# Chunk 5 of a squared-ReLU MLP as seven block products, with the splits of activations joined and two early weight loads

## The chip, the cores and the metric

The kernel runs on one core of one Trainium2 chip. The metric is the device time of one execution in microseconds (us), the median of several. The kernel before takes 505.07 us (three runs, 505.05 to 505.77). All times of single instructions come from one profiled execution of it, which took 505.25 us by itself; its span, from the first instruction to the last, is 503.5 us.

## The reference

One layer on 256 tokens of width 1024, all in float32: a conformer convolution and a sparse attention, mixed; a cross-attention on 256 memory tokens; an MLP with a squared ReLU; a final norm. Only the MLP is concerned here:

```
h  = h + CrossAttn(RMSNorm(h), RMSNorm(mem))
hf = RMSNorm(h) @ w_ff1            # 256 x 1024 times 1024 x 4096
h  = h + square(relu(hf)) @ w_ff2  # 256 x 4096 times 4096 x 1024
return RMSNorm(h)
```

## The kernel before

**Precision.** TensorE (PE) multiplies in fp32r, a rounded form of float32. Each operand is split into an upper part `hi` (a copy on ScalarE, ACT, that rounds) and the rest `lo` (a difference on VectorE, DVE). A product is three matmuls: hi by hi, hi by lo, lo by hi. So each weight of 1 MB (a chunk of 128 x 2048 numbers) costs DMA one load into a buffer `raw`, ACT two copies of 128x1024 and DVE two differences of 128x1024, ahead of the matmuls.

**Chunks.** The 4096 hidden columns are cut into 16 chunks of 256. For chunk c, `first(c, side)` makes its hidden values from the first weights `f1` of the chunk, one side (128 hidden columns) at a time: 24 matmuls into the PSUM bank `ps_f`. `activation` (a job in pieces, begun by `Hidden.after`) then applies Relu and Square and splits the result into `fs` (hi and lo). The second product, `half_of(c, half)`, multiplies it with the second weights `f2` of the chunk and adds into the banks `ps_p`, which hold sums over all chunks.

**Seven instead of eight.** The second product of a chunk is a 2 by 2 arrangement of blocks on each side of the product. Straightforwardly it takes eight block products of 512 columns, 24 matmuls. For the chunks in the table `SEVEN` it is done in the manner of Strassen and Winograd with seven, 21 matmuls. That needs sums of blocks of the weights (`sums`, made in `seven` by `outer` and `inner` on DVE and then split themselves) and differences of blocks of the activations (`fn`, in `activation`). The seven products take the weights in four pieces: `left` and `last` (parts of the weight itself), `outer` and `inner` (sums). Chunk 5 is not in the table before, so it takes eight, with two pieces 0 and 1 of the weight.

**The turn.** The loop over c up to 12 makes one turn out of `first(c + 2, 0)`, `half_of(c, 0)`, `first(c + 2, 1)`, `half_of(c, 1)`. Chunks 0 and 1 of `first` are made ahead of the loop.

**What sets the order.** All five instruction streams are written out by the program in the order of its calls; each engine does its own in that order and waits by semaphores. Weights come in the order `STREAM`: ..., f1 of chunks 0 and 1, f1 2, f2 0, f1 3, f2 1 and so on. Three buffers `raw` hold them; a load is issued on the queue of SyncE (SP) by `load()`, at the moment the last difference that reads an earlier one is written down (`high`, or the stage `inner` of `seven`). Its splits stand in `high_jobs` and `low_jobs`; `split_high` and `split_low` write out the next of each whenever `weights`, `split_ahead` or a tick between products asks. `HALVES` limits how many split halves may be there unused. A `Stage` has something to do `before` its copy (the sums); it is prepared when it stands second in line. The jobs of `activation` go on by one piece at each tick, each piece a few instructions up to its next `yield`.

**Memory and names.** `t8` and `w2` hand out work buffers from small rings; `cst` holds what stays. `raw51` to `raw53` are f1 of 0, 1 and 2, `raw54` is f2 of chunk 0; from there f1 and f2 alternate: `raw58` is f2 of chunk 2, `raw64` f2 of chunk 5, `raw70` f2 of chunk 8. In the kernel's listing, line 80 issues what DVE and PE do, 240 the copies of `seven`'s pieces, 263 the copies of other weights, 1166 the Relu straight from PSUM, 1170 and 1171 Relu and Square in place, 1190 the copy of the activations' upper parts, and 405 the copy of a bank whose sum is made in two banks (`merge`). Buffers such as `ki2`, `bias`, `score` and `zero_r` belong to earlier stages.

Of the kernel before, what the change touches and what calls it, by code (L numbers as in the profile page):

```python
# [16 lines left out]
P = 128  # L17
D = 1024
# [41 lines left out]
SEVEN = (2, 3, 4, 6, 7, 8, 9, 10, 11, 12)  # L60
JOINED = 13
BY_HALVES = tuple(("f1", i) for i in (4, 5, 6, 7))
# [52 lines left out]
def block_kernel(ctx, tc, x, xt, mem, memt, wst, wki, vecs, convw, gout, out):  # L115
# [23 lines left out]

    def bank(tag, bufs, name):  # L140
        return psum.tile([P, 512], F32, tag=tag, bufs=bufs, name=name)
# [19 lines left out]
    nload = [0]  # L161
    high_jobs, low_jobs = [], []

    def load(parts=1):
# [37 lines left out]
    class Stage:  # L202

        def __init__(self, key, high, before=None, slot=True):
            self.key, self.high, self.before, self.slot = key, high, before, slot
            if not slot:
                elsewhere.add(key)

        def prepare(self):
            if self.before:  # L210
                self.before()
                self.before = None

    def seven(key, c, raw):
# [15 lines left out]
        def stage(name, src_of, n, before=None):  # L230
            def high():
                src = src_of()
                if before:
# [16 lines left out]
            return Stage((*key, name), high, before, not before)  # L250

        return [stage("left", lambda: b[:, :, 0, :], 2), stage("last", lambda: flat[:, 3:4, :], 1),
                stage("outer", lambda: sums[0][:, 0:2, :], 2, outer), stage("inner", lambda: sums[0][:, 2:4, :], 2, inner)]

    def high(key, c, raw, ns, q, last):
# [184 lines left out]
    zero_r = cst.tile([P, 512], F32R, name="zero_r")  # L440
# [9 lines left out]
    ki2 = cst.tile([P, S], F32, name="ki2")  # L450
# [191 lines left out]
    bias = [cst.tile([P, P * (qb + 1)], F32, name=f"bias{qb}") for qb in range(2)]  # L642
# [22 lines left out]
    def index_scores():  # L665
# [4 lines left out]
        for qb in range(2):  # L670
            nk = P * (qb + 1)
            score = cst.tile([P, nk], F32, name=f"score{qb}")
# [490 lines left out]

    def activation(c, ct, ps, t, sh, sl):
        if ps.shape[1] == S:
            act(t[:, ct, :], ps, AF.Relu)  # L1166
        else:
            yield from merge(t[:, ct, :], ps)
            yield
            act(t[:, ct, :], t[:, ct, :], AF.Relu)  # L1170
        act(t[:, ct, :], t[:, ct, :], AF.Square)
        yield
        flat = t.rearrange("p k (r n) -> p (k r) n", r=2)
        if c not in SEVEN:
            cs = [(slice(2 * ct, 2 * ct + 2), flat[:, 2 * ct : 2 * ct + 2, :])]
        else:
            cs = [(slice(1, 3), flat[:, 2:4, :]) if ct else (slice(0, 1), flat[:, 0:1, :])]
        if ct and c < JOINED:
            n = w2(f"fn{c}", F32, (P, 4, P))
            if c in SEVEN:  # L1180
                dve.tensor_tensor(out=n[:, 0:2, :], in0=flat[:, 1:2, :].to_broadcast([P, 2, P]), in1=flat[:, 0:4:3, :],
                                  op=ALU.subtract)
                dve.tensor_tensor(out=n[:, 2, :], in0=flat[:, 0, :], in1=n[:, 1, :], op=ALU.subtract)
                dve.tensor_tensor(out=n[:, 3, :], in0=flat[:, 2, :], in1=n[:, 2, :], op=ALU.subtract)
                cs.append((slice(3, 7), n))
            else:
                dve.tensor_tensor(out=n[:, 0:2, :], in0=flat[:, 0:4:2, :], in1=flat[:, 1:4:2, :], op=ALU.subtract)
                cs.append((slice(4, 6), n[:, 0:2, :]))
        for js, src in cs:
            act(sh[:, js, :], src, AF.Copy)  # L1190
        yield
        for js, src in cs:
            dve.tensor_tensor(out=sl[:, js, :], in0=src, in1=sh[:, js, :].bitcast(F32), op=ALU.subtract)

    class Hidden:

        def __init__(self, c):
# [3 lines left out]
            self.t = w2(f"ft{c}", F32, (P, 2, S))  # L1201
# [7 lines left out]
        def row(self, k, rb):  # L1209
            return self.of(2 * k + rb)  # L1210
# [37 lines left out]
    TERMS = {"left": (("1", 0), ("2", 1)), "last": (("3", 6),), "outer": (("5", 4), ("7", 3)), "inner": (("6", 5), ("4", 2))}  # L1248
# [23 lines left out]
    def last_residual(rb, ps, lo, hi):  # L1272
        h = h_rm[:, lo // P : hi // P, rb, :]
        ps = by_tiles(ps)
        dve.scalar_tensor_tensor(out=h, in0=ps, scalar=r2[0][:, rb : rb + 1], in1=h, op0=ALU.mult, op1=ALU.add)

    def last_squares(rb, n, lo, hi):

        h = h_rm[:, lo // P : hi // P, rb, :]
# [163 lines left out]
```

## Time and profile before

| what | us |
|---|---|
| median of three runs | 505.07 |
| lowest and highest | 505.05, 505.77 |
| the profiled execution's own time | 505.25 |
| its span | 503.5 |

The profile's page gives for each engine the time it was busy (PE is TensorE's matmuls, PEld its weight loads, DVE VectorE, ACT ScalarE, POOL GpSimd), then the span in 40 slices, the DMA queues, and the chain of work that ended last. A row of a timeline reads: start, duration, engine, line, operation, output tile <- input tiles, partitions x elements and types, count; in brackets the engine's idle time just before it and what ended it. In it, rows with a count sum up neighbours of one form. A row of the chain of waits reads: start, duration, engine and what it did. Starts follow each other more closely than durations say, since instructions overlap by their beginnings and ends. A window row gives the busy time and the number of instructions for PE, PEld, DVE, ACT and POOL, then the granted clock of TensorE, the share of the DMA engines, and GB/s. The grouped rows give a group's count, its busy time with the mean in ns of one, and its idle time ahead. The lines are shown where the prediction uses them.

### The profile page before, as it was taken

To read this page: it belongs to the slowest core of one execution; us is meant where nothing else is said; L and a number is where in the kernel's file an instruction comes from. 1 tells how busy PE (TensorE), PEld (TensorE's weight loads), DVE (VectorE), ACT (ScalarE), POOL (GpSimd) and SP (SyncE) were. 2 spreads that over 40 slices of the span, in tenths; PEclk is the share of its full clock that TensorE was granted. 3 is DMA by queue.
4 is the path that set the end of the run, shared out by engine and by line. 5 is a ranking of instruction groups with operands and counts; after the bars stand their busy time and mean duration, and the time that the engine had idled before them with its cause. 6 is when DMAs were issued, how large, how long until landed. Compare 5 with 4: busy or idle time off the path is not lost.

```text
span 503.5 us, 8292 instructions
## 1 busy us (share of the span) xinstructions
PE 493.6 (98%) x3119; PEld 444.1 (88%) x3119; DVE 459.9 (91%) x858; ACT 349.1 (69%) x639; POOL 31.6 (6%) x49
## 2 busy tenths in 40 slices
PE   7999999999999999999999999999999999999995
PEld 5999998888888888888889999988989899988984
DVE  5999999999999799999988986888999899999994
ACT  7657777788656676668756667586777677777832
POOL 2002212221021100000000000000000000000000
PEclk9999999999999999999999999999999999999999
DMA  8949678899787744345645454368855645544602
GB/s 312 381 184 280 185 191 261 226 246 262 225 265 215 191 148 144 119 158 197 246 169 218 175 174 161 127 192 214 239 181 184 235 159 206 221 178 168 251 1 84
DMA packets 27225, 100.36 MB, mean 199 GB/s; under 512 B 10656, under 2 KB 11552, under 8 KB 17200
## 3 DMA queue, kind: packets, MB, share of 16 engines
q1 hardware_dynamic: 23120, 92.90, 53.4%
q0 software_dynamic: 3632, 6.59, 7.3%
q8 instruction: 24, 0.39, 0.3%
q10 hardware_dynamic: 432, 0.33, 0.2%
q14 instruction: 17, 0.14, 0.1%
HBM read 91.16 MB, written 1.05 MB: 183 GB/s over the span
## 4 chain that ended last, share of the span: by engine, by line
PE 62%; DVE 18%; ACT 7%; DMA 7%; issue 5%; POOLq 0%; POOL 0%; DVEq 0%; ACTq 0%
PE ps_conv L80 10%; DMA raw<-in_wst_dram 6%; PE ps_f L80 6%; DVE lo L80 5%; PE ps_ao L80 4%; PE ps_q L80 4%; PE ps_k L80 4%; PE ps_ga L80 4%; PE ps_gc L80 4%; PE ps_v L80 4%; PE ps_xo L80 3%; DVE sums L80 3%; PE ps_qi L80 2%; PE ps_xk L80 2%; PE ps_p L80 2%
## 5 line engine op out<-in xcount | busy, mean ns | idle before, releaser
L80 DVE TENSOR_TENSOR lo<-raw,hi 128x1024 fp32r<-128x1024 f32 x141 | 170.5, 1214 | 5.2 <-ACT hi L263 5.1
L263 ACT ACTIVATE hi<-raw 128x1024 fp32r<-128x1024 f32 x141 | 146.7, 1046 | 2.0 <-DMA raw<-in_wst_dram 2.0
L80 PE MATMUL ps_f<-ff_p,hi 128*128 128x256 f32 (+1 forms) x448 | 92.8, 299 | 0.6 <-ACT ft L1166 0.3
L80 DVE SCALAR_TENSOR_TENSOR acc<-u,cw,acc 128x234 f32<-128x234 f32 (+29 forms) x190 | 78.0, 461 | 0.3
L80 PEld LDWEIGHTS ps_f<-ff_p,hi 128*128 128x128 f32 x448 | 72.8, 191 | 5.8 <-ACT ft L1166 2.0
L80 PE MATMUL ps_f<-ff_p,lo 128*128 128x256 f32 x256 | 70.9, 282 | 0.0
L80 PEld LDWEIGHTS ps_f<-ff_p,lo 128*128 128x128 f32 x256 | 48.8, 191 | 0.6
L80 PE MATMUL ps_conv<-n_p,hi 128*128 128x256 f32 x224 | 41.0, 285 | 0.0
L80 PEld LDWEIGHTS ps_conv<-n_p,hi 128*128 128x128 f32 x224 | 34.9, 192 | 0.8 <-issue 0.7
L80 PE MATMUL ps_conv<-n_p,lo 128*128 128x256 f32 x112 | 31.7, 283 | 0.0
L588 POOL DMA_DIRECT2D acc<-products x25 | 21.6, 864 | 125.1 <-ACT products L587 50.1
L80 PE MATMUL ps_p<-hi,fs 128*128 128x512 f32 (+1 forms) x88 | 27.2, 372 | 0.0
L80 PE MATMUL ps_q<-n_p,hi 128*128 128x512 f32 x64 | 23.6, 406 | 0.0
L80 PE MATMUL ps_k<-n_p,hi 128*128 128x512 f32 x64 | 23.5, 407 | 0.0
L80 PE MATMUL ps_ao<-o_p,hi 128*128 128x512 f32 x64 | 22.6, 401 | 0.0
L80 PE MATMUL ps_co<-u_p,hi 128*128 128x512 f32 (+1 forms) x80 | 22.2, 351 | 0.0
L80 PE MATMUL ps_mix<-mix_p,hi 128*128 128x512 f32 (+1 forms) x80 | 22.2, 351 | 0.0
L80 PE MATMUL ps_ga<-n_p,hi 128*128 128x512 f32 x64 | 22.0, 396 | 0.0
L80 PE MATMUL ps_gc<-n_p,hi 128*128 128x512 f32 x64 | 22.0, 396 | 0.0
L587 ACT ACTIVATE products<-u,cw 128x231 f32<-128x231 f32 (+24 forms) x50 | 21.9, 489 | 0.0
L80 PEld LDWEIGHTS ps_conv<-n_p,lo 128*128 128x128 f32 x112 | 21.5, 192 | 0.0
L80 PE MATMUL ps_v<-hi,n_p 128*128 128x512 f32 x64 | 19.9, 389 | 0.0
(386 smaller groups left out, 1215.8 us busy)
## 6 DMA issues: line engine op xcount, KB each, us to landing
raw<-in_wst_dram SPq DMA_DIRECT2D x76, 1024.0 KB, 4.9
acc<-products POOLq DMA_DIRECT2D x25, 256.0 KB, 5.3
raw<-in_wst_dram SPq DMA_DIRECT2D x12, 512.0 KB, 7.6
x_rm<-in_x_dram SPq DMA_DIRECT2D x2, 512.0 KB, 4.2
mem_rm<-in_mem_dram SPq DMA_DIRECT2D x1, 1024.0 KB, 8.9
mem_t<-in_memt_dram SPq DMA_DIRECT2D x1, 1024.0 KB, 10.9
h_t<-in_xt_dram SPq DMA_DIRECT2D x1, 1024.0 KB, 7.0
h_rm<-turned SPq DMA_DIRECT2D x16, 64.0 KB, 5.6
```

Source lines behind the costliest of these rows:

```text
L80: return fn(*args, **kwargs)
L263: act(hi, raw[:, ns], AF.Copy)
L587: act(prod[:, a, s:], u[:, t, : S - s], AF.Copy, scale=cw[:, t, TAPS - 1 - s : TAPS - s])
L588: nc.gpsimd.dma_start(acc[:, ts, :], prod, accum_op=ALU.add)
```

## The change

- `SEVEN` gains chunk 5.
- `EXTRA = 2`: after the loads of the final gain, two more weight loads are issued (`raw55`, f1 of chunk 3, and `raw56`, f2 of chunk 1). They lie in `t8` buffers of their own, and their use issues no further load.
- `activation`: each side's Relu is done when its bank is ready; Square, the differences of blocks and the split follow once for both sides together, the split as one copy and one difference of 768 columns (chunks 0 and 1), 896 (those in `SEVEN`) or 512 (13 and 14). Before, a chunk was split in pieces. Chunk 15 goes by halves as it did. The differences lie in the tile `ft` itself, in place of `fn`.
- `seven`: the sums are made one instruction at a time: a `Stage` has a list of `steps`, and each `split_low` does one step of the first of three jobs that has any left. `load()` comes behind the last of these sums, not behind the difference of `inner`.
- Memory: `ft` comes from a new ring `w4`, `zero_r`, `ki2`, `bias` and `score` lie there too. Rows of a block pair are stored in the opposite order (`1 - rb`), with the indices in `TERMS` to match.

```diff
-SEVEN = (2, 3, 4, 6, 7, 8, 9, 10, 11, 12)
+SEVEN = (2, 3, 4, 5, 6, 7, 8, 9, 10, 11, 12)
+EXTRA = 2
...
-    def load(parts=1):
+    def load(parts=1, extra=False):
...
+        if extra:
+            early.add(c)
...
-        raw = t8(f"raw{c}", F32, (P, N_CHUNK)) if c in EARLY else raws.tile([P, N_CHUNK], F32, tag="raw", name=f"raw{c}")
+        raw = t8(f"raw{c}", F32, (P, N_CHUNK)) if c in early else raws.tile([P, N_CHUNK], F32, tag="raw", name=f"raw{c}")
...
-        def inner():
+        def inner(j):
             t = sums[0]
-            dve.tensor_tensor(out=t[:, 2, :], in0=t[:, 1, :], in1=flat[:, 0, :], op=ALU.add)
-            dve.tensor_tensor(out=t[:, 3, :], in0=t[:, 2, :], in1=flat[:, 2, :], op=ALU.add)
+            dve.tensor_tensor(out=t[:, j, :], in0=t[:, j - 1, :], in1=flat[:, 2 * j - 4, :], op=ALU.add)
+            if j == 3 and c not in early:
+                load()
...
-                    if name == "inner":
-                        load()
...
-            if last and c not in EARLY:
+            if last and c not in early:
                 load()
...
-            job.prepare()
+            while job.steps:
+                job.step()
             job.high()
...
-        if len(high_jobs) > 1:
-            high_jobs[1].prepare()
+        for job in high_jobs[:3]:
+            if job.steps:
+                job.step()
+                break
...
+    for _ in range(EXTRA):
+        load(extra=True)
...
+    def part(c, t, js, sh, sl):
+        act(sh[:, js, :], t, AF.Copy)
+        yield
+        dve.tensor_tensor(out=sl[:, js, :], in0=t, in1=sh[:, js, :].bitcast(F32), op=ALU.subtract)
...
     def activation(c, ct, ps, t, sh, sl):
...
+        if c == 15:
+            yield from by_halves(c, ct, ps, t, sh, sl)
+            return
+        yield from relu(ps, t[:, 2 * ct : 2 * ct + 2, :].rearrange("p r n -> p (r n)"))
+        if ct == 0:
+            return
+        act(t[:, 0:4, :], t[:, 0:4, :], AF.Square)
+        yield
+        js = slice(0, 4)
+        if c in SEVEN:
+
+            dve.tensor_tensor(out=t[:, 4:6, :], in0=t[:, 0:1, :].to_broadcast([P, 2, P]), in1=t[:, 1:3, :], op=ALU.subtract)
             yield
...
+            dve.tensor_tensor(out=t[:, 6, :], in0=t[:, 1, :], in1=t[:, 5, :], op=ALU.subtract)
+            yield
+            dve.tensor_tensor(out=t[:, 7, :], in0=t[:, 3, :], in1=t[:, 6, :], op=ALU.subtract)
+            yield
+            js = slice(1, 8)
+        elif c < JOINED:
+            dve.tensor_tensor(out=t[:, 4:6, :], in0=t[:, 1:4:2, :], in1=t[:, 0:4:2, :], op=ALU.subtract)
+            yield
+            js = slice(0, 6)
+        yield from part(c, t[:, js, :], slice(0, js.stop - js.start), sh, sl)
```

Two places show how the order moves. The first is ACT at the start of the MLP's loop, where chunk 0's activations (`ft_3719`, upper part in `fs_3718`) are split; `ft_3721` belongs to chunk 1, and `ps_f_3837` is the bank of chunk 2's first side. Before:

```order
L1190 ACTIVATE fs_3718<-ft_3719 128x256
L1170 ACTIVATE ft_3719<-ft_3719 128x256
L1171 ACTIVATE ft_3719<-ft_3719 128x256
L405 ACTIVATE ft_3721<-ps_f_3807 128x256
L263 ACTIVATE hi_1_3841<-raw_3604 128x1024
L1190 ACTIVATE fs_3718<-ft_3719 128x256
L1190 ACTIVATE fs_3718<-fn_3864 128x256
L1170 ACTIVATE ft_3721<-ft_3721 128x256
L1171 ACTIVATE ft_3721<-ft_3721 128x256
L405 ACTIVATE ft_3836<-ps_f_3837 128x256
L1190 ACTIVATE fs_3720<-ft_3721 128x256
```

And now, with `ps_f_3836` the bank of chunk 2's first side:

```order
L1180 ACTIVATE ft_3719<-ft_3719 128x256
L1201 ACTIVATE ft_3719<-ft_3719 128x512
L412 ACTIVATE ft_3721<-ps_f_3807 128x256
L267 ACTIVATE hi_1_3840<-raw_3600 128x1024
L1180 ACTIVATE ft_3721<-ft_3721 128x256
L412 ACTIVATE ft_3835<-ps_f_3836 128x256
L1183 ACTIVATE fs_3718<-ft_3719 128x768
```

Three copies into `fs_3718`, the last of them ahead of any read of chunk 2's bank, have become one, which stands behind the copy out of that bank. On DVE, at the same place, the difference for chunk 0 stands behind the mean squares of the norm:

```order
L81 TENSOR_TENSOR ft_3721<-ps_f_3807,ft_3721 128x256
L81 TENSOR_TENSOR ft_3835<-ps_f_3836,ft_3835 128x256
L81 TENSOR_SCALAR ms_ff<-ps_ff_3872 128x1
L81 TENSOR_SCALAR ms_ff<-ps_ff_3873 128x1
L81 RECIPROCAL ms_ff<-ms_ff 128x2
L81 TENSOR_TENSOR fs_3718<-ft_3719,fs_3718 128x768
```

Before, all three differences for chunk 0 stood ahead of the bank of chunk 2 and of the mean squares; one now follows both.

The second place is DVE in turn 7 of the loop, between one weight difference `lo_1` (the second half of f1 of chunk 9) and the next (of chunk 10), which are the rows just ahead of and just behind those shown, before and now. `raw_4531` is the buffer of f2 of chunk 7 and `raw_4660` that of chunk 8; `fs_4555` belongs to chunk 8's activations, `fs_4674` to chunk 9's. Before:

```order
L80 TENSOR_TENSOR sums_4642<-sums_4642,raw_4531 128x512 x2
L80 TENSOR_TENSOR fs_4555<-ft_4556,fs_4555 128x256
L80 TENSOR_TENSOR fs_4555<-fn_4653,fs_4555 128x512
L80 TENSOR_TENSOR outer_4664<-sums_4642,outer_4664 128x1024
L80 TENSOR_TENSOR inner_4678<-sums_4642,inner_4678 128x1024
L80 TENSOR_TENSOR lo_0_4710<-raw_4590,hi_0_4709 128x1024
L80 TENSOR_TENSOR fs_4674<-ft_4675,fs_4674 128x128
L80 TENSOR_TENSOR lo70left<-raw_4660,hi70left 128x1024
L80 TENSOR_TENSOR lo70last<-raw_4660,hi70last 128x512
L80 TENSOR_TENSOR sums_4759<-raw_4660 128x1024
L80 TENSOR_TENSOR fn_4770<-ft_4675 128x256
L80 TENSOR_TENSOR fn_4770<-ft_4675,fn_4770 128x128 x2
```

And now, with `raw_4499` and `raw_4610` in their places:

```order
L81 TENSOR_TENSOR sums_4566<-sums_4566,raw_4499 128x512
L81 TENSOR_TENSOR ft_4514<-ft_4514 128x128
L81 TENSOR_TENSOR outer_4615<-sums_4566,outer_4615 128x1024
L81 TENSOR_TENSOR ft_4514<-ft_4514 128x128
L81 TENSOR_TENSOR inner_4628<-sums_4566,inner_4628 128x1024
L81 TENSOR_TENSOR lo_0_4658<-raw_4502,hi_0_4657 128x1024
L81 TENSOR_TENSOR fs_4513<-ft_4514,fs_4513 128x896
L81 TENSOR_TENSOR lo70left<-raw_4610,hi70left 128x1024
L81 TENSOR_TENSOR sums_4677<-raw_4610 128x1024
L81 TENSOR_TENSOR lo70last<-raw_4610,hi70last 128x512
L81 TENSOR_TENSOR sums_4677<-sums_4677,raw_4610 128x512
L81 TENSOR_TENSOR ft_4625<-ft_4625 128x256
```

The first of the two sums for `inner` has moved ahead of the weight difference that begins the piece. The three splits of `fs`, of 256, 512 and 128 columns, have become one of 896, behind `lo_0`; the differences of blocks (`fn` before, `ft` now) are spread over the piece, and those of chunk 8 lie in it where before they lay ahead of it.

More of the change, by code (lines that the diff above doesn't have):

```diff
@@ L138, in w2, with w4 @@
         return work.tile(list(shape), dt, tag="w2", bufs=8, name=name)
+    def w4(name, dt=F32, shape=(P, KT, P)):
+        return work.tile(list(shape), dt, tag="w4", bufs=2, name=name)
     def bank(tag, bufs, name):
@@ L160, in block_kernel @@
     prepared, whole, elsewhere = {}, {}, set()
-    nload = [0]
+    nload, early = [0], set(EARLY)
     high_jobs, low_jobs = [], []
-    def load(parts=1):
+    def load(parts=1, extra=False):
         if nload[0] >= len(STREAM):
@@ L202, in block_kernel, with __init__, step @@
     class Stage:
-        def __init__(self, key, high, before=None, slot=True):
-            self.key, self.high, self.before, self.slot = key, high, before, slot
+        def __init__(self, key, high, steps=(), slot=True):
+            self.key, self.high, self.steps, self.slot = key, high, list(steps), slot
             if not slot:
                 elsewhere.add(key)
[L209 to L212, printed above, removed]
+        def step(self):
+            self.steps.pop(0)()
     def seven(key, c, raw):
@@ L223, in outer, with stage @@
                               in1=flat[:, 1:2, :].to_broadcast([P, 2, 512]), op=ALU.add)
-        def inner():
+        def inner(j):
             t = sums[0]
-            dve.tensor_tensor(out=t[:, 2, :], in0=t[:, 1, :], in1=flat[:, 0, :], op=ALU.add)
-            dve.tensor_tensor(out=t[:, 3, :], in0=t[:, 2, :], in1=flat[:, 2, :], op=ALU.add)
-        def stage(name, src_of, n, before=None):
+            dve.tensor_tensor(out=t[:, j, :], in0=t[:, j - 1, :], in1=flat[:, 2 * j - 4, :], op=ALU.add)
+            if j == 3 and c not in early:
+                load()
+        def stage(name, src_of, n, steps=()):
             def high():
                 src = src_of()
-                if before:
+                if steps:
                     both = t8(f"{name}{c}", F32R, (P, 2, 2, 512))
@@ L244, in low @@
                     prepared[(*key, name)] = (hi, lo)
-                    if name == "inner":
-                        load()
                 low_jobs.append(low)
-            return Stage((*key, name), high, before, not before)
+            return Stage((*key, name), high, steps, not steps)
         return [stage("left", lambda: b[:, :, 0, :], 2), stage("last", lambda: flat[:, 3:4, :], 1),
-                stage("outer", lambda: sums[0][:, 0:2, :], 2, outer), stage("inner", lambda: sums[0][:, 2:4, :], 2, inner)]
+                stage("outer", lambda: sums[0][:, 0:2, :], 2, (outer,)),
+                stage("inner", lambda: sums[0][:, 2:4, :], 2, (lambda: inner(2), lambda: inner(3)))]
     def high(key, c, raw, ns, q, last):
@@ L640, in block_kernel @@
     wi = cst.tile([P, 2, 8], F32, name="wi")
-    bias = [cst.tile([P, P * (qb + 1)], F32, name=f"bias{qb}") for qb in range(2)]
+    bias = [picked[:, :P], picked[:, P : 3 * P]]
     def causal(t, qb, value):
@@ L1162, in block_kernel @@
     start(ff_scale())
-    def activation(c, ct, ps, t, sh, sl):
[L1165 to L1168, printed above, removed]
-            yield
[L1170 to L1193, printed above, removed]
@@ new lines, in relu, with by_halves @@
+    def relu(ps, t):
+        if ps.shape[1] == S:
+            act(t, ps, AF.Relu)
+        else:
+            yield from merge(t, ps)
+            yield
+            act(t, t, AF.Relu)
+    def part(c, t, js, sh, sl):
+        act(sh[:, js, :], t, AF.Copy)
+        yield
+        dve.tensor_tensor(out=sl[:, js, :], in0=t, in1=sh[:, js, :].bitcast(F32), op=ALU.subtract)
+    def by_halves(c, ct, ps, t, sh, sl):
+        js = slice(2 * ct, 2 * ct + 2)
+        yield from relu(ps, t[:, js, :].rearrange("p r n -> p (r n)"))
+        act(t[:, js, :], t[:, js, :], AF.Square)
+        yield
+        yield from part(c, t[:, js, :], js, sh, sl)
@@ L1246, in half_of @@
             tick()
-    TERMS = {"left": (("1", 0), ("2", 1)), "last": (("3", 6),), "outer": (("5", 4), ("7", 3)), "inner": (("6", 5), ("4", 2))}
+    TERMS = {"left": (("1", 0), ("2", 2)), "last": (("3", 6),), "outer": (("5", 4), ("7", 3)), "inner": (("6", 5), ("4", 1))}
     def seventh(x, name):
@@ L1272, in last_residual @@
     def last_residual(rb, ps, lo, hi):
[L1273 removed]
+        h = h_rm[:, lo // P : hi // P, 1 - rb, :]
         ps = by_tiles(ps)
[L1275 removed]
+        dve.scalar_tensor_tensor(out=h, in0=ps, scalar=r2[0][:, 1 - rb : 2 - rb], in1=h, op0=ALU.mult, op1=ALU.add)
     def last_squares(rb, n, lo, hi):
[L1279 removed]
+        h = h_rm[:, lo // P : hi // P, 1 - rb, :]
         junk = w2(f"junk_o{rb}{n}")
```

19 lines of the change are left out of this document (11 added, 8 removed).

## The prediction

> **What bounds the kernel now.** I read the page first, then the windows, then the chain of waits and the timelines of the MLP, which begins near 323 us and is the only stage that the change touches.
>
> ```profile
> span 503.5 us, 8292 instructions
> PE 493.6 (98%) x3119; PEld 444.1 (88%) x3119; DVE 459.9 (91%) x858; ACT 349.1 (69%) x639; POOL 31.6 (6%) x49
> PEclk9999999999999999999999999999999999999999
> ...
> core 0: us, PE busy (x) PEld busy (x) DVE busy (x) ACT busy (x) POOL busy (x), PEclk, DMA share, GB/s
> 424.50:435.50 11.00, 11.00 (x73) 10.05 (x72) 10.81 (x16) 8.06 (x14) 0.00 (x0) 1.00 0.49 185
> ```
>
> PE is busy without a break at the full clock over a whole turn of the MLP, so the end moves only by matmuls removed and by PE's waits. But in that window DVE stands at 10.81 of 11.00 us, and ACT at 8.06. PE's own turn is shorter, by the chain of waits where PE runs freely:
>
> ```profile
> 397.90 2.75 PE ps_p L80 x12
> 400.64 2.87 PE ps_f L80 x24
> 403.52 2.07 PE ps_p L80 x9
> 405.58 2.89 PE ps_f L80 x24
> ```
>
> Two first products (2.87 each), one half with nine matmuls left of it (2.07) and one with twelve (2.75): 10.56 us for a seven-product turn. DVE's turn can be seen in a pair of instructions eleven microseconds apart, each the last weight difference of a turn; I call its end D, and S is the start of the first product behind it on PE.
>
> ```profile
> 410.58 1.22 DVE L80 TENSOR_TENSOR lo<-raw,hi 128x1024 fp32r<-128x1024 f32 x1
> 415.98 0.40 PE L80 MATMUL ps_f<-ff_p,hi 128*128 128x256 f32 x2
> 421.62 1.22 DVE L80 TENSOR_TENSOR lo<-raw,hi 128x1024 fp32r<-128x1024 f32 x1
> 454.59 1.22 DVE L80 TENSOR_TENSOR lo<-raw,hi 128x1024 fp32r<-128x1024 f32 x1
> 457.80 0.39 PE L80 MATMUL ps_p<-lo76last,fs 128*128 128x512 f32 x1
> 458.03 0.39 PE L80 MATMUL ps_p<-hi76last,fs 128*128 128x512 f32 x1
> 458.55 0.50 PE L80 MATMUL ps_f<-ff_p,hi 128*128 128x256 f32 x2
> ```
>
> D goes from 411.80 to 455.81 in four turns, 11.00 each. PE is ahead of nothing but DVE's stock: at 411.80 the stock (S less D) is 4.18 us, four turns later PE wants to start at 458.26 (458.03 and one matmul of 0.23), which leaves 2.45, and it starts at 458.55. That is a wait of 0.29, and the first two matmuls behind it take 0.50 where they take 0.40 without one: 0.39 in all. The chain of waits names what ended it, and two more like it:
>
> ```profile
> 371.18 1.06 ACT inner L240
> ...
> 393.38 1.06 ACT hi66left L240
> ...
> 457.17 1.06 ACT inner L240
> ...
> 371.88 0.39 PE L80 MATMUL ps_p<-hi60last,fs 128*128 128x512 f32 x1
> ...
> 372.56 0.39 PE L80 MATMUL ps_f<-ff_p,hi 128*128 128x256 f32 x1 [0.29 <-ACT ft L1166]
> ...
> 394.24 0.39 PE L80 MATMUL ps_p<-hi,fs 128*128 128x512 f32 x1
> 394.76 0.38 PE L80 MATMUL ps_f<-ff_p,hi 128*128 128x256 f32 x1
> ```
>
> PE needs the one free bank of ps_f, which the Relu on ACT (ft) empties, and that stands behind a copy of `inner`, which needs DVE's sums, or of a fresh load. Start to start less one matmul: 0.45, 0.29 and 0.29, plus 0.10 or so each: **1.33 us are all that PE waits here**. The Relu behind 457.17 is done some 0.32 after that copy, 2.7 us after D; whenever the stock is under that, PE waits. Chunk 5, with eight products, has no sums for DVE (1.13 + 2 x 0.60 by the steps between starts, worked out below) and splits of 2.26 instead of 4.0: some 4 us less, and this is where the stock is filled up again, to 4.18 still at 411.80.
>
> **The change part by part.** Sums are against the profiled execution's own 505.25 us, 0.18 above the median of the runs.
>
> *Matmuls.* Chunk 5 by seven products: three matmuls of 512 columns fewer, 3 x 0.23 = **-0.69**.
>
> *The old waits*: **-1.33**, since the order that made them is gone; what replaces them is counted below.
>
> *The split of chunk 0 in one go.* The first product of the second weights needs fs0. These rows stand at its place:
>
> ```profile
> 336.79 0.39 PE L80 MATMUL ps_p<-hi,fs 128*128 128x512 f32 x1
> 337.25 0.61 PE L80 MATMUL ps_p<-hi,fs 128*128 128x512 f32 x2
> 338.16 0.50 PE L80 MATMUL ps_ff<-onesd,sums_ff 128*128 128x2 f32 x4
> 337.28 0.36 ACT L405 ACTIVATE ft<-ps_f 128x256 f32<-128x256 f32 x1
> L1190 ACT ACTIVATE fs<-fn 128x512 fp32r<-128x512 f32 x10 | 6.3, 633 | 9.5 <-DVE fn L80 9.4
> L80 DVE TENSOR_TENSOR fs<-fn,fs 128x512 fp32r<-128x512 f32 x10 | 6.9, 685 | 0.4 <-ACT fs L1190 0.4
> L263 ACT ACTIVATE hi<-raw 128x1024 fp32r<-128x1024 f32 x39 | 40.5, 1047 | 1.2 <-DMA raw<-in_wst_dram 1.2
> L80 DVE TENSOR_TENSOR lo<-raw,hi 128x1024 fp32r<-128x1024 f32 x39 | 47.1, 1217 | 2.1 <-ACT hi L263 2.1
> ```
>
> Now fs0 is complete when PE arrives at 336.79. In the new order ACT's copy of 768 columns stands behind the copy of ps_f20, whose matmuls end only at 336.79; that copy (0.36) is over near 337.2 to 337.3, and 768 columns lie halfway between 0.633 and 1.047, 0.84: fs0's upper part is there at 338.04. DVE's part starts then (its two short statistics are done) and lies halfway between 0.685 and 1.217, 0.95: 339.0. PE has the four small matmuls of ps_ff to do first (0.36, to 337.15), its first two matmuls need the upper part alone, and the third starts at about 339.15 where without a wait it would start at 337.25 + 0.36 = 337.61: **+1.5**. Bounds: 0 if what PE has to do before fs0 is longer than I read, 1.6 with the whole chain a semaphore later. I take 1.5, since every piece is a row or lies between two. This delays all behind it, loads too.
>
> *The later turns.* What changes is DVE's list. Per turn it now has six instructions of 1024 columns, three of 512, 256 and twice 128, and 896. Between starts 1024 take 1.13 and 512 take 0.60 (417.75 to 418.89 to 419.49 below); from 419.49 to 421.62 are 2.13, which leaves 1.00 for 256 and twice 128 where each waits for the one ahead, so 0.75 where other work lies between them; 896 by the line through 512 and 1024 take 1.0: 6.78 + 1.81 + 0.75 + 1.0 = 10.4 us, now **below** PE's 10.56. But DVE is not free to run them at will:
>
> ```profile
> 411.82 4.81 DMA raw<-in_wst_dram
> 413.15 0.33 SPq L176 DMA_DIRECT2D raw<-in_wst_dram  x1
> 416.65 1.07 ACT hi70left L240
> ...
> 417.75 1.23 DVE L80 TENSOR_TENSOR lo70left<-raw,hi70left 128x1024 fp32r<-128x1024 f32 x1
> 418.89 0.69 DVE L80 TENSOR_TENSOR lo70last<-raw,hi70last 128x512 fp32r<-128x512 f32 x1
> 419.49 1.22 DVE L80 TENSOR_TENSOR sums<-raw 128x1024 f32<-128x1024 f32 x1
> 464.60 1.22 DVE L80 TENSOR_TENSOR lo<-raw,hi 128x1024 fp32r<-128x1024 f32 x1
> ```
>
> The load of the next second weights is issued the moment D is past (411.80, 411.82), because the buffer comes free there and there are three as before; it lands 4.81 later, ACT copies it, and DVE's difference starts at D + 5.95. Behind it, in the new order (left, sums, last, sums, the 256, lo), come 1.14 + 1.13 + 0.60 + 0.60 + 0.34 + 1.22 = 5.03 to the next D. This loop is **10.98 us**, whatever DVE saves elsewhere; I use 10.95, since the landing itself varies. So the stock still falls by 10.95 - 10.56 = 0.39 a turn, and chunk 5 no longer fills it.
>
> Where it starts: D of turn 2 comes 2.7 us (a copy, a merge, a copy and lo) after the last first product of turn 1, and S is a half, a first product and a half further on, 2.75 + 2.87 + 2.07 = 7.69: stock 5.0. In turn 3 the 896 columns (1.0) lie inside the loop's second part: 11.98, stock 3.5. Then 3.1, 2.7, 2.35, and 1.95 in turn 7. Where it hurts: only the last sum (0.60) instead of two stands ahead of `inner`, so the Relu is done at D + 0.60 + 0.03 + 1.06 + 0.28 + 0.05 = D + 2.02 instead of 2.70. Turn 7 thus waits 0.07 + 0.10, turns 8 to 11 the loop's excess of 0.39 each (1.56). Turn 12's D comes sooner, as before (464.60 is 10.01 behind 454.59), so the stock there is 2.02 + 10.56 - 10.01 = 2.5 or 2.6; but a Relu now stands behind two copies of a load that lands 4.9 after D: 4.9 + 2 x 1.05 + 0.3 = 7.3, and PE wants its bank after 24 small and six large matmuls, 2.5 + 2.87 + 1.37 = D + 6.8: about 0.45 + 0.10. **+2.3** in all; with a loop of 10.90 some 1.4 less, with 11.05 as much more.
>
> *At no cost:* the order of rows and the tables, which only rename; the moved buffers, whose old users end long before; and the two early loads, since PE waits for no load before 393.38, so that sooner landings there are worth nothing, and from the third load behind them every load again has the distance of before. Were they in another load's way, it would be once, at rival 3's price: 0 to 1.4.
>
> Sum: -0.69 - 1.33 + 1.5 + 2.3 = **+1.8**, that is 507.0 for the profiled execution and 506.8 for the median.
>
> Two rules beside this. The Trainium skill, "VectorE: DVE Perf Modes", section "The TRN2 errata — SBUF-src ops pay a fixed extra latency per instruction", says that each such instruction pays a fixed time, so that few long ones beat many short ones. The rows agree: 0.60 for 512 against 1.13 for 1024 leave 0.07 fixed. By that rule alone the change gains on DVE, and the time would be rival 1's; by the loop of 10.98 the gain becomes idle time of DVE ahead of a load. The Trainium skill, "DMA: Bandwidth & Descriptors", section "Queues, rings and completion order", says that a DMA engine takes its descriptors in ring order; by it a follower would not slow the load ahead, and rival 3 falls; the row 411.82 agrees, with 4.81 for a load whose follower was issued 1.33 later.
>
> **The rivals.** *1: the stock lasts.* If DVE's own 10.4 us set the turn, not the load, or the loop is under 10.7, the stock of 3.5 in turn 3 never falls to 2.0 and the 2.3 are absent: 505.25 - 0.69 - 1.33 + 1.5 = 504.7, by the median 504.5; with a rest of half a microsecond 505.0. For it: DVE at 10.81 of 11.00 may have been the bound itself. Against: the load's chain of 417.75 alone gives 10.95. *2: as 1, and the early wait is hidden too* (an ACT copy that comes sooner): 503.0. Against it stand the rows at 336.79. *3, a larger loss: the following load, now issued 0.6 behind the leader (after one sum instead of two) and not 1.33 (413.15), slows it.*
>
> ```profile
> 357.37 6.24 DMA raw<-in_wst_dram
> ```
>
> A load has taken 6.24 where others were under way. That would be 1.4 more in each turn; three of the eight turns behind turn 3 make 506.8 + 4.2 = 511. It decides as soon as two loads share the engines so that the first lands past D + 5.2.
>
> **How the numbers follow.** Forecast (506.0 to 508.2): 0.60. Rival 1, with rests to 0.5: 0.27. Rival 2: 0.08. Rival 3: 0.05. The median's 0.2%, 1.0 us, is about what a measurement can tell from no change, so 504.1 to 506.1 is "same". Slower is the forecast (but for 0.02 of it) and rival 3, 0.62 with some rounding; same is rival 1 and that rest, 0.29; faster 0.09. The range from 504.4 to 508.2 holds the forecast and nearly all of rival 1, and leaves out rival 2 and 3; the forecast's own is 506.0 to 508.2.
>
> **What would show it.** PE's start of the first product of chunk 15 sums up all but the tail:
>
> ```profile
> 473.47 0.40 PE L80 MATMUL ps_f<-ff_p,hi 128*128 128x256 f32 x2
> ```
>
> It should come near 475.2. On the way there: PE's third ps_p matmul near 339.1, with fs as releaser on DVE; no wait on `ft` before turn 7, then 0.3 to 0.4 before each first product of turns 7 to 11, and one of 0.45 in turn 12; D every 10.95 us with DVE waiting up to 0.45 us at the left difference for a load. If DVE never waits there, and D comes every 10.5, rival 1 is right. I am wrong altogether if PE waits on weights instead of on `ft`, or if the loads land more than 5.2 us after their issue.

## The result, and the profile after

The changed kernel takes 507.71 us (median of 6 runs, 507.31 to 509.09) where the kernel before takes 505.06 (6 runs, 504.92 to 505.77): a ratio of 1.0056, with a 95% interval of 1.0043 to 1.0068. It is slower by half a per cent, and the whole interval lies above 1 (the prediction took 0.2% as the least that a measurement can tell). Its profiled execution took 507.45, with a span of 505.7 where the one before had 503.5.

The page's first lines:

```profile
span 505.7 us, 8232 instructions
PE 494.2 (98%) x3116; PEld 443.3 (88%) x3116; DVE 459.9 (91%) x837; ACT 344.9 (68%) x598; POOL 31.6 (6%) x49
```

Three matmuls, 21 instructions of DVE and 41 of ACT are fewer; DVE's busy time is the same 459.9. As an estimate, chunk 5's sums and splits add some 4.1 (the prediction's 2.33 and 1.74), and the joined splits save about as much: 0.36 in each of eleven turns (10.81 busy in a turn before, 10.45 now). The span grew by 2.2 with fewer matmuls, so the time went into PE's waits. The first stands where chunk 0's activations are split. Timelines of PE, ACT and DVE there, each row with its start, duration and, in brackets, the idle time ahead and what ended it:

```profile
338.04 0.50 PE L81 MATMUL ps_p<-hi,fs 128*128 128x512 f32 x1 [0.86 <-ACT fs L1183]
...
339.04 0.73 PE L81 MATMUL ps_p<-hi,fs 128*128 128x512 f32 x2 [0.26 <-DVE fs L81]
```
```profile
336.88 0.38 ACT L412 ACTIVATE ft<-ps_f 128x256 f32<-128x256 f32 x1 [1.14 <-PE ps_f L81]
337.16 0.83 ACT L1183 ACTIVATE fs<-ft 128x768 fp32r<-128x768 f32 x1
```
```profile
335.24 0.42 DVE L81 TENSOR_TENSOR ft<-ft 128x256 f32<-128x256 f32 x1
...
337.88 0.17 DVE L81 RECIPROCAL ms_ff<-ms_ff 128x2 f32<-128x2 f32 x1
338.02 0.96 DVE L81 TENSOR_TENSOR fs<-ft,fs 128x768 fp32r<-128x768 f32 x1
```

What the copy of `fs` reads was ready at 335.66 (the block differences at 335.24 and their 0.42), and ACT had nothing to do for 1.14 us; but the copy stood behind one that waited for PE. So PE waited for ACT and ACT for PE, in the order of the code alone. From start to start, less a matmul of 0.23 each and less the 0.10 that was there before, this costs 1.60.

The second place is the later turns. The timeline of PE around one of six such waits:

```profile
415.68 0.39 PE L81 MATMUL ps_p<-hi68last,fs 128*128 128x512 f32 x1
416.34 0.50 PE L81 MATMUL ps_f<-ff_p,hi 128*128 128x256 f32 x2 [0.28 <-ACT ft L1176]
...
475.63 0.51 PE L81 MATMUL ps_f<-ff_p,hi 128*128 128x256 f32 x2 [0.24 <-ACT ft L1176]
```

From 415.68 to 416.34 are 0.66, 0.43 more than a matmul, and 0.10 follow. The same sum in turns 7 to 12 gives 0.54, 0.48, 0.43, 0.39, 0.47 and 0.50: 2.81 us where the kernel before lost 1.33 in three. PE waits for the Relu, which stands on ACT behind the copy of `inner`, and that copy waits for a sum on DVE (ACT's timeline):

```profile
414.96 1.06 ACT L245 ACTIVATE inner<-sums 128x1024 fp32r<-128x1024 f32 x1 [2.21 <-DVE sums L81]
415.92 0.36 ACT L1176 ACTIVATE ft<-ps_f 128x256 f32<-128x256 f32 x1
```

And DVE, whose lateness is behind this, waits itself:

```profile
413.11 1.21 DVE L81 TENSOR_TENSOR lo<-raw,hi 128x1024 fp32r<-128x1024 f32 x1
414.24 0.68 DVE L81 TENSOR_TENSOR sums<-sums,raw 128x512 f32<-128x512 f32 x1
...
418.65 1.08 DVE L81 TENSOR_TENSOR fs<-ft,fs 128x896 fp32r<-128x896 f32 x1
420.32 1.23 DVE L81 TENSOR_TENSOR lo70left<-raw,hi70left 128x1024 fp32r<-128x1024 f32 x1 [0.58 <-ACT hi70left L245]
...
424.14 1.22 DVE L81 TENSOR_TENSOR lo<-raw,hi 128x1024 fp32r<-128x1024 f32 x1
```

In the chain of waits of the same kernel (start, duration, what) the load is what stands between:

```profile
414.35 4.86 DMA raw<-in_wst_dram
...
419.23 1.07 ACT hi70left L245
```

D, the end of the weight difference, is 414.33 (413.11 and its 1.21, each rounded). The load is issued at 414.35, lands 4.86 later, is copied, and DVE takes it up at 420.32, at D + 5.99. The next D comes at 425.36: a loop of 11.03. The window of one turn (busy us of PE, PEld, DVE, ACT and POOL) shows that DVE's own work is shorter than that:

```profile
core 0: us, PE busy (x) PEld busy (x) DVE busy (x) ACT busy (x) POOL busy (x), PEclk, DMA share, GB/s
403.23:414.33 11.10, 11.10 (x74) 10.00 (x73) 10.45 (x14) 7.61 (x10) 0.00 (x0) 1.00 0.52 190
```

### The profile page after: what moved, and what is told of

It reads as the page before. It is cut to its first block, busy times and chain, and to the rows that moved or that the text cites. A ratio compares the mean times of both kernels' runs of the same rounds, so it can differ in the third digit from the quotient of the medians.

```text
span 505.7 us, 8232 instructions
## 1 busy us (share of the span) xinstructions
PE 494.2 (98%) x3116; PEld 443.3 (88%) x3116; DVE 459.9 (91%) x837; ACT 344.9 (68%) x598; POOL 31.6 (6%) x49
## 4 chain that ended last, share of the span: by engine, by line
PE 74%; DVE 9%; DMA 8%; ACT 4%; issue 4%; POOL 0%; POOLq 0%; SPq 0%; DVEq 0%; ACTq 0%
PE ps_conv L81 10%; PE ps_f L81 8%; DMA raw<-in_wst_dram 7%; PE ps_co L81 4%; PE ps_mix L81 4%; PE ps_ao L81 4%; PE ps_p L81 4%; PE ps_q L81 4%; PE ps_k L81 4%; PE ps_ga L81 4%; PE ps_gc L81 4%; PE ps_v L81 4%; PE ps_xo L81 3%; DVE sums L81 3%; PE ps_qi L81 2%
## 5 line engine op out<-in xcount | busy, mean ns | idle before, releaser
L81 DVE TENSOR_TENSOR lo<-raw,hi 128x1024 fp32r<-128x1024 f32 x139 | 168.0, 1214 | 4.3 <-ACT hi L267 4.1
L267 ACT ACTIVATE hi<-raw 128x1024 fp32r<-128x1024 f32 x139 | 144.6, 1047 | 1.5 <-DMA raw<-in_wst_dram 0.8
L245 ACT ACTIVATE inner<-sums 128x1024 fp32r<-128x1024 f32 x11 | 11.7, 1062 | 22.0 <-DVE sums L81 22.0
L81 PE MATMUL ps_p<-hi,fs 128*128 128x512 f32 (+1 forms) x72 | 21.9, 370 | 1.1 <-ACT fs L1183 0.9
```

What stands on the lines that cost most here:

```text
L81: return fn(*args, **kwargs)
L245: act(hi, src, AF.Copy)
L267: act(hi, raw[:, ns], AF.Copy)
```

## The experiments

Theory A, the prediction's: in the later turns the loop over the load (D, issue, landing, copy, differences, next D) sets the turn, and near 338 the order of ACT and DVE. Rival B: DVE's work in all sets the turn. Rival C: the joined splits or the early loads are to blame, and chunk 5 by seven products is a gain. All times are medians, with the ratio to the kernel before, run on the same chip; that kernel's own median was 505.2 to 505.5 in these runs.

**1. One yield less for chunk 0.**

```diff
             dve.tensor_tensor(out=t[:, 4:6, :], in0=t[:, 1:4:2, :], in1=t[:, 0:4:2, :], op=ALU.subtract)
-            yield
+            if c:
+                yield
```

> The changed kernel with one yield less: for chunk 0 the copy of the 768 columns follows at once behind their difference, so on ScalarE it stands ahead of the copy out of chunk 2's bank. My theory: the 1.6 us that TensorE waits near 338 are that order alone; they vanish, and the later waits (2.8 in all), which hang on the load loop of 11.0 us, stay as they are, since everything moves sooner together: 507.7 - 1.6 = 506.1. Rival: fs0 is late for another reason (the sums of the norm, a weight), then 507.5 or more.

506.62 us, 1.0025 (1.0008 to 1.0042). The profiled executions differ by 1.4 (506.03 and 507.45). PE's wait for ACT's copy is gone, by its order alone. Half a microsecond was left: the copy now waits for DVE's block differences, which on DVE stand behind a weight difference and the sums of the norm, and DVE in turn waits for the copy. Timelines of ACT and DVE:

```profile
335.64 0.85 ACT L1183 ACTIVATE fs<-ft 128x768 fp32r<-128x768 f32 x1 [0.25 <-DVE ft L81]
```
```profile
335.19 0.42 DVE L81 TENSOR_TENSOR ft<-ft 128x256 f32<-128x256 f32 x1
...
336.52 0.96 DVE L81 TENSOR_TENSOR fs<-ft,fs 128x768 fp32r<-128x768 f32 x1 [0.58 <-ACT fs L1183]
```

Of 1.60, 0.53 remain at this place; the waits of the later turns stay (2.4 instead of 2.9, with one of 0.07 in turn 6 counted in both). What follows: the early loss is the order of ACT and DVE, and the later one is there without it.

**2. The sums over two jobs instead of three**, so that one sum moves behind D; and **3.** the same with experiment 1.

```diff
-        for job in high_jobs[:3]:
+        for job in high_jobs[:2]:
```

> The changed kernel with the sums of the second weights spread over the first two instead of the first three jobs in line: the same instructions, but one sum of 512 columns stands behind the last weight difference of a turn and not ahead of it. My theory: the loop from that difference over the load back to it is 0.6 shorter, 10.4 instead of 11.0, under TensorE's 10.56, so the stock of time no longer falls; the price is that the copy of inner, and with it the Relu behind it, comes at D + 3.9 instead of D + 2.0, and the stock after turn 3 is about 4.1, so hardly any late wait is left (0 to 0.6 instead of 2.8). The early wait stays: 507.7 - 2.2 to 2.8 = 504.9 to 505.5. Rival (VectorE's work in all, or the clock of another engine, sets the turn): the work is the same, so the late waits stay, 507.5; or the later Relu makes TensorE wait more, above 508.

> Both edits together: the copy for chunk 0 sooner and the sums over two jobs. My theory: the two losses are independent, 507.7 - 1.6 - 2.2 to 2.8 = 503.3 to 503.9, faster than the kernel before. Rival: one of the two losses hides the other, so that 505 to 506 are left.

512.32 us, 1.0133 (1.0119 to 1.0148), and 511.78, 1.0125 (1.0109 to 1.0140). The expectation fell. Timelines of DVE and ACT:

```profile
425.44 1.22 DVE L81 TENSOR_TENSOR lo<-raw,hi 128x1024 fp32r<-128x1024 f32 x1
...
428.52 0.68 DVE L81 TENSOR_TENSOR sums<-sums,raw 128x512 f32<-128x512 f32 x1
...
430.32 1.23 DVE L81 TENSOR_TENSOR inner<-sums,inner 128x1024 fp32r<-128x1024 f32 x1 [0.93 <-ACT inner L245]
...
433.69 1.22 DVE L81 TENSOR_TENSOR lo72left<-raw,hi72left 128x1024 fp32r<-128x1024 f32 x1
...
436.89 1.22 DVE L81 TENSOR_TENSOR lo<-raw,hi 128x1024 fp32r<-128x1024 f32 x1
```
```profile
429.23 1.06 ACT L245 ACTIVATE inner<-sums 128x1024 fp32r<-128x1024 f32 x1 [2.95 <-DVE sums L81]
```

The last sum now stands nearly next to the difference of `inner`, which needs ACT's copy of that sum; DVE waits 0.93 for it, and its turn is 11.45 (436.89 less 425.44) without any wait for a load (433.69). The order that shortened one loop made another, from DVE to ACT and back. The runs do not contradict A, but they are no support for it either: I had counted the sum's move and not what then follows it.

**4. Chunk 5 by eight products again**, the rest as changed.

```diff
-SEVEN = (2, 3, 4, 5, 6, 7, 8, 9, 10, 11, 12)
+SEVEN = (2, 3, 4, 6, 7, 8, 9, 10, 11, 12)
```

> The changed kernel with chunk 5 by eight products again, all else as changed. My theory: 0.69 of matmuls more, but the two turns around chunk 5 take VectorE's loop 20.0 instead of 22.0 us and TensorE 21.8 instead of 21.1: the stock is 2.7 higher from turn 6 on, at 4.8, and falls to 2.7 by turn 11, above the 2.0 from which TensorE waits. So all late waits go (2.8): 507.7 + 0.7 - 2.8 = 505.6, of which 1.6 is the early wait. Rival (chunk 5 as seven is a plain gain, and the loss lies in the joined splits): 508.4.

506.80 us, 1.0024 (1.0016 to 1.0033). It is faster than with seven products although it has three matmuls more, which speaks against C; but the gain is 0.9 (0.7 by the spans) and not 2.1. In turns 11 and 12 waits of 0.36 and 0.38 are left, and one in turn 5, which I had left out:

```profile
394.68 1.06 ACT L245 ACTIVATE hi66left<-raw 128x1024 fp32r<-128x1024 f32 x1 [3.69 <-DMA raw<-in_wst_dram]
```
```profile
396.06 0.38 PE L81 MATMUL ps_f<-ff_p,hi 128*128 128x256 f32 x1 [0.51 <-ACT ft L1176]
```

It is the wait that the kernel before had at 394.76: the Relu stands behind the copy of a load that is issued late. It costs 0.77.

**5. Less for DVE ahead of its wait.** The lower part of the activations of chunks 5 to 12 is left out, and the upper part is multiplied in its place.

```diff
-        dve.tensor_tensor(out=sl[:, js, :], in0=t, in1=sh[:, js, :].bitcast(F32), op=ALU.subtract)
+        if c not in SEVEN or c < 5:
+            dve.tensor_tensor(out=sl[:, js, :], in0=t, in1=sh[:, js, :].bitcast(F32), op=ALU.subtract)
...
-            return self.hi[:, j, :], self.lo[:, j, :]
+            return self.hi[:, j, :], (self.hi if self.c in SEVEN and self.c >= 5 else self.lo)[:, j, :]
```

> The changed kernel without the difference of 896 columns that gives the lower part of the activations, for chunks 5 to 12: their lower part is left out, the upper part is multiplied in its place, so the matmuls are as many. VectorE has 1.0 us less to do in each of these turns, ahead of its wait for the load. My theory (the loop over the load sets the turn): VectorE only waits 1.0 longer at the left piece, its last difference comes every 11.0 as before, and TensorE waits as before: 507.7, within 0.4. Rival (VectorE's work in all sets the turn): 9.4 us a turn, no late wait, 504.9.

507.62 us, 1.0047 (1.0032 to 1.0062): no gain from 1.0 us less work of DVE in eight turns. The timeline of DVE shows where it went:

```profile
413.98 1.22 DVE L81 TENSOR_TENSOR lo<-raw,hi 128x1024 fp32r<-128x1024 f32 x1
...
421.14 1.23 DVE L81 TENSOR_TENSOR lo70left<-raw,hi70left 128x1024 fp32r<-128x1024 f32 x1 [1.53 <-ACT hi70left L245]
```

The wait grew from 0.58 to 1.53, and PE's late waits are 3.5 in all, not fewer. That they are more goes with one load in turn 5 of this execution, which landed after 5.81 and made that one loop 12.0; in turns 6 to 11 D comes every 11.0, as before. B is out.

**6. No early loads.**

```diff
-EXTRA = 2
+EXTRA = 0
```

> The changed kernel without the two early loads. My theory: they change no wait, 507.7 within 0.4, perhaps with another first wait. Rival: the two loads are what the later turns live on, so the stock at turn 3 is smaller by a load and TensorE waits in all turns from 3 on, 4 turns more of 0.45: 509.5. Second rival: they cost time by being in the way, 507.0 or less.

508.01 us, 1.0056 (1.0041 to 1.0071): as with them. They do not cause the loss. By the traces they raise the stock of turn 3 from 2.71 to 3.44, and without them turn 6 waits too (0.39); but the loops of this execution were a little shorter (10.95 in the mean), and PE's late waits come to 3.0 where they were 2.9. A gain of a few tenths is not excluded.

**7. The kernel before with chunk 5 by seven products** and nothing else.

```diff
-SEVEN = (2, 3, 4, 6, 7, 8, 9, 10, 11, 12)
+SEVEN = (2, 3, 4, 5, 6, 7, 8, 9, 10, 11, 12)
```

> The kernel before with chunk 5 by seven products and nothing else. My theory: its turn of VectorE is 11.0, too, and its Relu needs a stock of 2.7; without the 4 us that chunk 5 leaves to VectorE, TensorE waits in turn 5 a little and in turns 6 to 11 by 0.45 each, and some 0.5 in turn 12: waits of 3.9 instead of 1.3, less 0.69 of matmuls: 505.1 + 1.9 = 507.0. Rival (chunk 5 as seven is a plain gain): 504.4.

507.53 us, 1.0044 (1.0029 to 1.0059). PE waits in each of turns 3 to 11, 4.7 in all where 3.9 were expected. This one line of the change makes the kernel before about as slow as the whole change does, so C is out: chunk 5 by seven products is a loss in either kernel, by the medians 2.2 us in the kernel before and 0.9 in the changed one. What the joined splits are to blame for is the 1.60 near 338; with them the later waits are 2.9 and not 4.7.

**8. A fourth weight buffer**: one early load that calls for its successor, and every fourth load from there on into a larger work buffer.

```diff
-EXTRA = 2
+EXTRA = 1
...
-        if extra:
-            early.add(c)
+        if extra or (c > 55 and c % 4 == 3 and c < 79):
+            deep.add(c)
...
-        raw = t8(f"raw{c}", F32, (P, N_CHUNK)) if c in early else raws.tile([P, N_CHUNK], F32, tag="raw", name=f"raw{c}")
+        raw = t8(f"raw{c}", F32, (P, N_CHUNK)) if c in early or c in deep else raws.tile([P, N_CHUNK], F32, tag="raw", name=f"raw{c}")
```

> The changed kernel with a fourth weight buffer in rotation: one early load that does call for its successor, and every fourth load from there on into one of the larger work buffers. The second weights are then issued half a turn sooner, behind the sums of the turn before, and land before VectorE asks for them. My theory: the loop over the load is cut, VectorE's turn is its own 10.4, the stock stays at 3.5, and the late waits are gone: 507.7 - 2.8 = 504.9, with the early wait left. Rival: something else than the landing sets the 11.0 (VectorE's work, ScalarE), 507.5; or the work buffers come free too late and the loads wait for them, over 508.

505.30 us, 1.0000 (0.9990 to 1.0009). All late waits are gone; what is left of waiting is the 1.60 near 338. A row of the waits (who waits for whom: us in all, how often, the longest), the timeline of DVE and the window of two turns:

```profile
ACT ft L1176 <- PE ps_f L81: 19.9, 23, 1.4
```
```profile
416.54 1.08 DVE L81 TENSOR_TENSOR fs<-ft,fs 128x896 fp32r<-128x896 f32 x1
417.54 1.22 DVE L81 TENSOR_TENSOR lo70left<-raw,hi70left 128x1024 fp32r<-128x1024 f32 x1
```
```profile
401.46:422.58 21.12, 21.12 (x140) 19.39 (x139) 20.90 (x27) 15.23 (x20) 0.00 (x0) 1.00 0.53 200
```

Now ACT waits for PE and never PE for ACT in these turns; DVE goes on from `fs` to the left piece without a pause; two turns take 21.12, twice PE's 10.56, with DVE's own 10.45 a turn just inside. No work was taken away, only the load's place in the loop. PE's last matmul starts 2.78 sooner (496.55 and 499.33); the span is 2.5 shorter and the median 2.4, since 0.27 more pass behind that matmul and some 0.3 more outside of the span.

**9. The load issued later by its call.** The call for the second weights' load moves behind the last sum.

```diff
             if j == 3 and c not in early:
-                load()
+                for _ in range(1 + len(owed)):
+                    load()
+                owed.clear()
...
             if last and c not in early:
-                load()
+                if 60 < c < 76:
+                    owed.append(c)
+                else:
+                    load()
```

> The changed kernel with the load of the second weights, from that of chunk 5 to that of chunk 12, issued one sum of 512 columns (0.60) later: behind the last sum for inner, together with the load that follows it. No engine's work is changed. My theory: the loop grows by 0.60 in eight turns, and since the stock is nearly gone there, TensorE waits all of it: some 1.06 in each of turns 6 to 11 and 1.1 in turn 12 in place of 0.4 to 0.5 each, 507.7 + 4 to 5 = 512 or so. Rival (VectorE's work sets the turn, with 0.5 to spare): 508.5 at most. If the two loads together slow each other, more than 513.

507.63 us, 1.0048 (1.0034 to 1.0062), not 512. The edit didn't do what it should. In the timelines of DVE and SP the load is still issued when D is past:

```profile
413.45 1.22 DVE L81 TENSOR_TENSOR lo<-raw,hi 128x1024 fp32r<-128x1024 f32 x1
```
```profile
414.70 0.33 SPq L182 DMA_DIRECT2D raw<-in_wst_dram  x1
```

SP has nothing else to do and waits for the buffer's last reader, not for the place of the call. D is 414.67 (413.45 and its 1.22), the issue 0.03 behind it. So this run says nothing on A; it says that the place of the call alone, which the change moved too, does not set the issue. The kernel before shows the same: there the call for the next load stands behind the difference of `inner` (L80 at 415.11), and the load is issued at 413.15, when DVE's sums are done.

**10. The buffer held longer.** One column of it is read behind the last sum, in eight turns.

```diff
+                for r in late:
+                    dve.tensor_tensor(out=held_by, in0=r[:, 0:1], in1=t[:, 3, 0:1], op=ALU.add)
+                    load()
+                late.clear()
                 load()
...
-            if last and c not in early:
+            if 60 < c < 76 and last:
+                late.append(raw)
+            elif last and c not in early:
                 load()
```

> The changed kernel with one more instruction in eight turns: VectorE reads one column of the first weights' buffer behind the last sum for inner, so the buffer is held and the load of the second weights can only be issued some 0.75 to 0.9 later (in the run before this one a later call alone did not delay the issue, which hangs on the buffer and not on the place of the call). The added read is one column; it lies where VectorE waits half a microsecond for the load anyway. My theory: the loop grows by 0.75 to 0.9 from turn 5 on, and TensorE waits all of it in turns 6 to 12, on top of 0.4 to 0.5: 507.7 + 5 to 6.5 = 512.7 to 514. Rival (VectorE's work in all sets the turn): 508.5 at most.

512.40 us, 1.0138 (1.0120 to 1.0156). The timelines of DVE and of SP (two loads in one row):

```profile
415.04 1.22 DVE L81 TENSOR_TENSOR lo<-raw,hi 128x1024 fp32r<-128x1024 f32 x1
...
416.89 0.16 DVE L81 TENSOR_TENSOR held_by<-raw,sums 128x1 f32<-128x1 f32 x1
...
422.87 1.23 DVE L81 TENSOR_TENSOR lo70left<-raw,hi70left 128x1024 fp32r<-128x1024 f32 x1 [1.01 <-ACT hi70left L249]
...
426.69 1.22 DVE L81 TENSOR_TENSOR lo<-raw,hi 128x1024 fp32r<-128x1024 f32 x1
```
```profile
416.93 0.80 SPq L182 DMA_DIRECT2D raw<-in_wst_dram  x2
```

An instruction of 0.16 us delays the issue by 0.65 (416.93 on SP, where D is 416.26). The loop is 11.65 instead of 11.03, and the waits of turns 5 to 12 are 7.6 in all instead of 2.9: 4.7 more, and the median is 4.7 higher. A little under what I expected, because the delay was 0.65 and not 0.75 to 0.9. This and experiment 8 move the loop in both directions, with DVE's own work the same but for the 0.16, and PE's waits follow by the size: A is shown.

**11. Both cures: the fourth buffer, and chunk 0 split without yields up to the copy; 12.** the same with the last yield gone, too.

```diff
...
         act(t[:, 0:4, :], t[:, 0:4, :], AF.Square)
-        yield
+        if c:
+            yield
...
```

> The fourth weight buffer together with the split of chunk 0 made at once: Square, the difference, and the copy of 768 columns follow each other without a yield, so that the copy stands ahead of the copies out of both later banks. My theory: the fourth buffer alone left only the early wait of 1.6; with it gone TensorE waits nowhere in the loop, and the 0.69 of matmuls and the 1.3 of old waits are gained: 505.3 - 1.5 = 503.8, faster than the kernel before by 1.3 to 1.6. Rival: TensorE, sooner by 1.5, overtakes the loads at the start of the loop and waits there for what it gained, 505.0.

> The fourth weight buffer, and for chunk 0 all of Square, difference, copy and the lower part's difference without a yield, so that on VectorE the lower part stands ahead of the sums of the norm and of a weight difference. My theory: in the run with the fourth buffer and the earlier copy, 1.1 of wait was left ahead of the third product, whose lower part stood behind those two; it goes, unless the weight difference that now comes 1.3 later is missed: 504.35 - 1.1 = 503.3. Rival: VectorE's wait for the copy delays the weights of chunk 2 and TensorE waits there instead, 504.3.

504.35 us, 0.9983 (0.9974 to 0.9992), and 504.62, 0.9986 (0.9977 to 0.9995). Both are faster than both kernels: the first by 3.4 us than the changed one, and by 1.0 than the kernel before, with an interval that leaves out 1. That is less than I had expected (503.8 and 503.3), since the early wait only moved. Timelines of PE and DVE, two rows of the first and two of the second:

```profile
338.11 0.73 PE L81 MATMUL ps_p<-hi,fs 128*128 128x512 f32 x2 [0.78 <-DVE fs L81]
```
```profile
334.23 0.43 DVE L81 TENSOR_TENSOR ft<-ft 128x256 f32<-128x256 f32 x1 [1.41 <-ACT ft L1201]
```
```profile
339.07 0.61 PE L81 MATMUL ps_ff<-onesd,sums_ff 128*128 128x2 f32 x4 [0.88 <-DVE sums_ff L81]
```
```profile
335.53 0.96 DVE L81 TENSOR_TENSOR fs<-ft,fs 128x768 fp32r<-128x768 f32 x1 [0.91 <-ACT fs L1183]
```

With the difference late, PE waits for it; with it early, the sums of the norm are late. DVE itself stands idle there for ACT, 1.41 us ahead of the block differences and, in the second, 0.91 more ahead of the lower part. Whether some other order leaves no wait stays open.

## Why the prediction was right

*Direction and places.* Slower was forecast at 506.8, in a range of 504.4 to 508.2; measured are 507.71. That range held rival 1's time, too, so it is the places that tell: each of the four terms has the sign that was forecast, where it was forecast. The first product of chunk 15 starts at 475.63 (475.2 forecast), and DVE waits 0.50 to 0.66 at the left difference of turns 3 to 11 (up to 0.45 forecast).

*Matmuls*, -0.69: three fewer, as said. *Old waits*, -1.33: those of turns 3 and 5 are gone; the third, in turn 11, stands where it stood and is counted among the later turns here.

*Chunk 0's split*, +1.5 forecast and 1.60 found. The third matmul starts at 339.04, forecast 339.15; the copy took 0.83 (0.84) and the difference 0.96 (0.95), so the line through two measured sizes held. The remaining 0.1 is the pause of the first matmuls behind a wait, which I had not counted here. Experiment 1 shows the cause.

*The later turns*, +2.3 forecast and 2.81 found: this term was mis-sized. The loop was put at 10.95 and is 11.02 in the mean of turns 4 to 11 (D from 370.18 in turn 3 to 458.32), because the landing takes 4.77 to 4.92, 4.84 in the mean, where I took 4.81, and because I rounded 10.98 down. In the four turns up to turn 7 the loop was 11.04 in the mean, with two landings of 4.92. So the stock, 3.44 in turn 3, was 1.57 in turn 7 and not 1.95, and that turn waited 0.54 and not 0.17; turns 8 to 11 waited 1.77 instead of 1.56, and turn 12 0.50 instead of 0.55. The Relu's need of D + 2.02 was right: 414.33 and 416.34 are 2.01 apart. The sum of the terms found, -0.69 - 1.33 + 1.60 + 2.81 and 0.07 in turn 6, is 2.46, where the spans differ by 2.2. Of this 0.26, 0.11 lie ahead of the MLP, which begins at 322.71 and not at 322.82, and 0.08 behind the last matmul; no term forecast them, so the sum came nearer by luck than its terms. For the profiled execution 507.0 was forecast and 507.45 came; the median lies another 0.26 above it, where before it lay 0.18 below its own.

*What was costed at nothing.* The early loads cost nothing and are worth nothing that the time shows (experiment 6), but not for the reason given: the stock of 3.44 in turn 3 includes 0.73 from them. The order of rows and buffers leaves no wait that the trace names.

*Rivals.* Rival 1, that DVE's own 10.4 us set the turn: its premise on the work was right, 10.45, and DVE nonetheless came every 11.0, because it waited for the load; experiments 5, 8 and 10 refute it. In the kernel before, DVE's list and the load's loop were of about one length: there it waits less than 0.1 at the left difference of 417.75, and its 10.81 of 11.00 looked like a bound. DVE's busy time in a turn fell from 10.81 to 10.45, and the wait ahead of the left piece grew to 0.58. The rule of the Trainium skill, "VectorE: DVE Perf Modes", section "The TRN2 errata — SBUF-src ops pay a fixed extra latency per instruction", is that few long instructions beat many short ones. The rows agree with it: the splits of 256, 512 and 128 columns took 0.42, 0.68 and 0.28, the one of 896 takes 1.08. Rival 3, that a follower close behind slows a load: the follower came 0.60 behind the leader, which landed after 4.86 in turn 7, and in experiment 10, with the follower 0.43 behind it, after 4.83. These numbers agree with the ring order of the Trainium skill, "DMA: Bandwidth & Descriptors", section "Queues, rings and completion order". Single loads took longer all the same, none of them in the changed kernel's later turns: 6.20 in the kernel before (issued at 398.90) and 5.81 in experiment 5, with no other load under way ahead of them. Others with a follower at the same distance took 4.8, so the distance is not what slowed them; what did stays open. Rival 2 had no support: the early wait was there.

## What to carry to other kernels

Where an engine is busy for 98% of a turn, ask whether it is the bound or whether its list happens to be as long as a loop that runs through it: follow one buffer from its last reader over the load and the splits back to that reader, and compare the sum with the turn. Work taken off ahead of such a loop's wait turns into idle time; here one more buffer in rotation shortened the turn itself, and one more reader of the buffer made it longer. And before a slack turn is spent on fewer matmuls, add up what it had been paying back: here eight products in one chunk filled a stock that later turns lived on. Of the six that wait in the changed kernel, five do not wait in the one before.

## What I had not expected of the hardware

A load's issue follows the buffer and not the program: the call moved by an instruction changed nothing, the issue came 0.03 behind D (experiment 9); an added read of one column moved it by 0.65 us (experiment 10). A copy on ACT of what DVE has just made, which DVE then needs, costs DVE 0.93 us of waiting at 128x1024 where little else lies between (experiment 2). And in experiment 8 the profiled execution's own time is 2.1 us above its span (505.27 and 503.2) where it was 1.8 before; what lies outside of the span was not followed up; these 0.3 us are a part of why that run is at 1.0000 rather than below.
